# Hybrid trunk on one core: small plain-precision products as stacked parts in one single-rate product, norm sums from parts in two passes

## The chip, the cores and the metric

The kernel runs on one core of a Trainium2 chip. The time is that of the device for one execution, in microseconds (us); the number compared is the median of several executions. A profile is one further execution, recorded by the hardware profiler.

A core has engines that run side by side, each through its own list of instructions in order: TensorE (PE: matrix products into PSUM, with weight loads, PEld), VectorE (DVE), ScalarE (ACT), GpSimd (POOL) and SyncE (SP, which here issues the transfers). They wait for one another by semaphores.

## The reference

One layer of a hybrid trunk, for a prompt of 256 tokens with 16 learned meta tokens ahead of it, and for 8 sample tokens, which continue from given states. All in float32, width 2048:

```python
def decoder_layer(x, pos, s_ret, s_hg, prompt, ...):
    x = layer_norm(ALPHA * x + 0.5 * swiglu(x, f1_g, f1_u, f1_d), ln1_g, ln1_b)
    m, s_ret, s_hg = token_mixer(x, pos, s_ret, s_hg, prompt, w_in, lb, hg_norm_g, w_out)
    x = layer_norm(ALPHA * x + m, ln2_g, ln2_b)
    x = layer_norm(ALPHA * x + 0.5 * swiglu(x, f2_g, f2_u, f2_d), ln3_g, ln3_b)
    return x, s_ret, s_hg

# token_mixer: ten projections of x, then two branches
#   retention: 8 heads of 256, per-head decay; S_new = decay * S + k_dec^T v, and o = (q k^T * D) v + q_dec S
#   HGRN2: 16 heads of 128, forget gate f per feature, k = 1 - f;
#          S_new = exp(b_last) * S + k_dec^T v, and o likewise with the products of the gates
# y = sigmoid(a_r) * norm(o_r) * silu(g_r) + sigmoid(a_h) * norm(o_h) * silu(g_h);  return y @ w_out, s_ret, s_hg
```

The outputs are the tokens after the layer and the states of both branches, for the prompt and for each sample. The first 16 tokens of the prompt (the meta tokens) are computed as a chunk of their own, and are left out of the token output.

## The kernel before, in words

Features lie on the 128 partitions and tokens in the columns: 280 columns (16 meta, 256 prompt, 8 sample), or 264 where the meta tokens are no longer needed. `T` is 280, `TL` 264, `LP` 272.

**Products.** A plain float32 product shows as two records in the profile, one of float32r operands as one record; the latter is called single rate here. The kernel splits a value x in an upper part hi, which ACT makes as a copy cast to float32r, and a lower part lo = x - hi, which DVE makes as float32r (`split`, L188 to L190). `dense` (L175) makes each block of a weight product from three single-rate products, hi·hi, hi·lo and lo·hi (L182 to L184). Its weights come in units of 8 blocks of 128x128: `stream` (L143) issues the load of a unit on SP's queue, ACT casts it to `whi` (L159), DVE subtracts to `wlo` (L160); three units are in flight. `sums` (L192, L195) adds over the partitions in two passes, from an upper and a lower part, with a matrix of ones.

**Stages.** ffn 1 (up, down), then the first layer norm, the mixer, the product with `w_out` and the second norm, ffn 2, the third norm.

**Norms.** `Norm` gathers the residual in 16 tiles `d`. `shift` (L277) takes the mean of the first tile over its partitions, the product `pc` (L280), as an approximate mean that is subtracted from every tile; it is called from a hook after block k = 6 of the second output group. The running sums of d and its square are tiles `ls1` and `ls2` (`ls` in the profile), which `stats` (L310) adds over partitions in two products `p1` and `p2` (L313, L314). For norms 1 and 2 the next stage's first group of products (`first`, L322) starts with the values that are not yet normalised; `stats` is called from a hook after its block k = 4, and `normalise` (L343) rewrites `xh` and `xl` (L350, L351) behind it. The third norm ends in `finish`.

**Mixer.** For each unit u = 0 to 7 the groups of projections run, and between their blocks `pump` (after every k) takes steps of two generators, `mix_hg` (two HGRN2 heads) and `mix_ret` (one retention head). A `yield n` says how many k's to wait for the next step. In `mix_hg`, keys and values are transposed; the 16 meta tokens' keys and values go to `km` (L735) and `vm` (L656), tiles of 128 rows that are zero below row 16, and their state is the plain product `pst<-vm,km` (L751). Two chunks of 128 follow (L752, L753). In `mix_ret`, the last 24 tokens' values are in `vt2`; the states (`psr`, L852) are single rate already, and their third block of 24 tokens is one product in which parts stand below one another (`ks2`, `vs2`: rows 0, 32 and 64). The output `por` (L897) is the sum of three products with the scores: two blocks of 128 tokens and a third, `vt2` with `scr2`, of 16 columns. Values are centred (`centre`, L789) between.

**Order.** TensorE runs in the order in which the program is written. DVE and ACT are ordered by a scheduler by priorities and its own estimates, so a step of the mixer may stand behind weight splits or steps of the other branch on them. All transfers of weights, states and tables are issued by SP.

Of the kernel before, what the change touches and what calls it, by code (L numbers as in the profile page):

```python
# [10 lines left out]
F32 = mybir.dt.float32  # L11
# [90 lines left out]
def trunk(ctx: ExitStack, tc: tile.TileContext, A, O):  # L102
# [127 lines left out]
    class Norm:  # L230
# [5 lines left out]
        def __init__(self, which, n, whole, lead):  # L236
# [4 lines left out]
            if lead:  # L241
                self.bs = lnb[:, which - 1]
                split(self.bs[:, 0, :], self.bs[:, 1, :], self.b)

        def row(self, name):
            return row_tile(name)[:, : self.n]

# [29 lines left out]
        def shift(self):  # L277
            n = self.n
            pc = mx_bank("pc")
            nc.tensor.matmul(pc[:, :n], ones, self.d[0], start=True, stop=True)  # L280
# [29 lines left out]
        def stats(self):  # L310
            n = self.n
            p1, p2 = mx_bank("p1"), mx_bank("p2")
            nc.tensor.matmul(p1[:, :n], ones, self.s1, start=True, stop=True)  # L313
            nc.tensor.matmul(p2[:, :n], ones, self.s2, start=True, stop=True)  # L314
            self.mean = self.row("lnc")
            nc.scalar.mul(self.mean, p1[:, :n], 1.0 / D)
            var = self.row("lnq")
            mul(var, self.mean, self.mean)
            nc.vector.scalar_tensor_tensor(out=var, in0=p2[:, :n], scalar=1.0 / D, in1=var, op0=ALU.mult, op1=ALU.subtract)
            self.r = rsqrt(self.row, var, 1.0, (eps_h if self.whole else eps_l))  # L320

        def first(self, block, outs):  # L322

            n = self.n

            def hook(k):
                if k == 4:
                    self.stats()
# [12 lines left out]
            return ys  # L341
# [54 lines left out]
    def ffn(i, block, w_dn, which, before=None):  # L396
# [3 lines left out]
        with tc.tile_pool(name=f"h{i}", bufs=1) as hp:  # L400
# [23 lines left out]
            for m in range(KC):  # L424
                o = acc_bank(f"dn{m}")
                norm.ahead(m)
                dense(block, FC, [o], hh, hl, cols, (lambda k: k == 6 and norm.shift()) if m == 1 else None)
                norm.chunk(m, o[:, :n])
        return norm

# [34 lines left out]
    with tc.tile_pool(name="yp", bufs=1) as yp:  # L465
        yh, yl = [None] * KC, [None] * KC
        with tc.tile_pool(name="mp", bufs=1) as mp:
# [38 lines left out]
            km = tmp("km", (P, P))  # L506
            vm = tmp("vm", (P, 2, 2, P))
            vt2 = tmp("vt2", (P, 2, P))
            scr2 = tmp("scr2", (P, NMETA))


            ks2 = tmp("ks2", (P, 2, P), dt=F32R)
            vs2 = tmp("vs2", (P, 2, P), dt=F32R)
            for z in (km, vm, vt2, scr2):
                nc.gpsimd.memset(z, 0.0)
            for z in (ks2, vs2):
                nc.scalar.copy(z.rearrange("p c f -> p (c f)"), vm.rearrange("p h b f -> p (h b f)")[:, : 2 * P])
            threads = []

            def pump(_=None):  # L520
# [86 lines left out]
            NB2 = LP - 2 * P  # L607
            BLOCKS = ((0, P), (P, P), (2 * P, T - 2 * P))

            def rows_out(src, width, tag):  # L610

                scr = drp.tile([NS, width], F32, tag=tag + "d", name=tag + "d")
                nc.sync.dma_start(scr, src)
                return scr
# [11 lines left out]
            def mix_hg(u, f, k, q, v):  # L626
# [23 lines left out]
                for h in range(2):  # L650

                    pt = mx_bank("pt")
                    for b, (t0, n) in enumerate(((NMETA, P), (NMETA + P, P), (0, NMETA), (T - NMETA, NMETA))):
                        nc.tensor.transpose(pt[:n, b * P : (b + 1) * P], v[:, h, t0 : t0 + n], ident)
                    nc.scalar.copy(vt[:, h], pt[:, : 2 * P].rearrange("p (b f) -> p b f", b=2))
                    nc.scalar.copy(vm[:NMETA, h], pt[:NMETA, 2 * P :].rearrange("p (b f) -> p b f", b=2))  # L656
                    vrow.append(rows_out(vm[8:16, h, 1, :], P, f"vh{h}"))
                    yield 1
                yield 9 if u else 5
                pd = mx_bank("pd")  # L660
# [68 lines left out]
                for h in range(2):  # L729
# [5 lines left out]
                    nc.scalar.copy(km[:NMETA, :], pt[:NMETA, 2 * P : 3 * P])  # L735
# [12 lines left out]

                    S = tmp("Sh", (P, 3, P))
                    pst = mx_bank("pst")  # L750
                    nc.tensor.matmul(pst[:, 0:P], km, vm[:, h, 0, :], start=True, stop=True)  # L751
                    nc.tensor.matmul(pst[:, P : 2 * P], kt[:, 0, :], vt[:, h, 0, :], start=True, stop=True)  # L752
                    nc.tensor.matmul(pst[:, 2 * P : 3 * P], kt[:, 1, :], vt[:, h, 1, :], start=True, stop=True)  # L753
                    nc.scalar.copy(S[:, 0, :], pst[:, :P])
# [33 lines left out]

            def centre(x):  # L789

                n = x.shape[1]
                m = tmp("cen", (P, n))
                nc.vector.tensor_reduce(out=m, in_=x, op=ALU.add, axis=mybir.AxisListType.X)
                nc.vector.tensor_scalar(out=m, in0=m, scalar1=1.0 / 256, scalar2=None, op0=ALU.mult)
                nc.vector.tensor_tensor(out=x, in0=x, in1=m.unsqueeze(2).to_broadcast([P, n, 256]), op=ALU.subtract)

            def mix_ret(u, q, k, v):
                vt = tmp("vtr", (P, 2, 2, P))
# [6 lines left out]
                for c in range(2):  # L805
# [7 lines left out]
                    nc.scalar.copy(vs2[third[0], c, :], vt2[:NB, c, :])  # L813
                    nc.scalar.copy(vs2[third[2], c, :], vt2[:NB, c, :])
                    sub(vs2[third[1], c, :], vt2[:NB, c, :], vs2[third[0], c, :].bitcast(F32))
                    yield 1
                    pt = mx_bank("pt")
                    for b, (t0, n) in enumerate(BLOCKS):
# [104 lines left out]
        for gn, grp in enumerate(out_groups()):  # L923
            outs = [acc_bank(f"wo{m}") for m in grp]
            norm2.ahead(grp[0])
            dense(block, KC, outs, yh, yl, slice(0, TL), (lambda k: k == 6 and norm2.shift()) if gn == 1 else None)
            for m, o in zip(grp, outs):
                norm2.chunk(m, o[:, :TL])

# [115 lines left out]
```

## Time and profile before

| | us |
|---|---|
| median of 3 runs (2813.01 to 2816.25) | 2814.84 |
| the profiled execution | 2817.09 |
| its span | 2815.0 |
| TensorE busy (22664 records) | 2797.8, 99% |
| DVE busy (2842) | 1721.1, 61% |
| ACT busy (2034) | 1354.6, 48% |
| POOL busy (42) | 4.3 |

The mean clock granted to TensorE in the profiled execution is 0.998. A line of the timeline reads: start us, length us, engine, line, operation, output tile <- input tiles, sizes, count, and in brackets the engine's idle time before it with what ended that. The length of a matmul is longer than the distance to the next start, as matmuls overlap. A line of waits reads: engine, the tile and line that waited, the tile and line waited for, us in total, times, longest us. Buffer numbers are left out of tile names. float32r is written f32 for matmuls; a plain product shows as two records (x2).

### The profile page before, as it was taken

The page shows a single profiled execution, that of the slowest core. Times are in us where ns is not written, and L with a number is a line of the kernel's source. Part 1 is how long each engine was busy: PE and PEld are TensorE (multiplying, and loading weights), DVE is VectorE, ACT ScalarE, POOL GpSimd, SP SyncE. Part 2 cuts the span into 40 slices and gives each one's busy share as a digit, 9 for nine tenths or more (in the row PEclk, how much of TensorE's full clock was granted, in tenths as well). Part 3 has the DMA queues.
Part 4 walks back from the last instruction along what each step waited for, and adds up shares of the span by engine and source line. Part 5 has one row for each costly group of instructions (what it writes and reads, how often), then busy time and mean ns, then how long its engine had stood idle before and what let it go on. Part 6 is the DMA issues. An engine that isn't in the chain of part 4 may idle for free.

```text
span 2815.0 us, 54477 instructions
## 1 busy us (share of the span) xinstructions
PE 2797.8 (99%) x22664; PEld 2765.0 (98%) x22664; DVE 1721.1 (61%) x2842; ACT 1354.6 (48%) x2034; POOL 4.3 (0%) x42
## 2 busy tenths in 40 slices
PE   9999999999999999999999999999999999999999
PEld 9999999999999999999999999999999999999998
DVE  5444444464478777777777777775884444446444
ACT  4443344433355565656565656564554444444333
POOL 0000000000000000000000000000000000000000
PEclk9999999999999999999999999999999999999999
DMA  6555555555555675757575757575555555565654
GB/s 224 172 171 168 172 172 171 168 170 173 169 175 173 226 249 177 250 175 254 175 253 175 254 174 254 175 250 172 177 179 181 184 182 180 180 183 179 181 180 140
DMA packets 154439, 536.26 MB, mean 190 GB/s; under 512 B 17680, under 2 KB 25424, under 8 KB 154192
## 3 DMA queue, kind: packets, MB, share of 16 engines
q1 hardware_dynamic: 154048, 532.50, 59.1%
q8 instruction: 177, 2.90, 0.4%
q14 instruction: 70, 0.57, 0.1%
q10 hardware_dynamic: 144, 0.29, 0.0%
HBM read 502.12 MB, written 30.61 MB: 189 GB/s over the span
## 4 chain that ended last, share of the span: by engine, by line
PE 97%; DVE 1%; ACT 1%; DMA 1%; issue 0%; SPq 0%; ACTq 0%; DVEq 0%
PE up L183 12%; PE up L184 12%; PE up L182 12%; PE dn L182 6%; PE dn L183 6%; PE dn L184 6%; PE pj_v_r L182 1%; PE pj_f L182 1%; PE pj_k_r L182 1%; PE pj_f L183 1%; PE pj_k_r L183 1%; PE pj_v_r L183 1%; PE pj_v_r L184 1%; PE pj_f L184 1%; PE pj_g_r L182 1%; PE pj_k_r L184 1%
## 5 line engine op out<-in xcount | busy, mean ns | idle before, releaser
L160 DVE TENSOR_TENSOR wlo<-raw,whi 128x1024 fp32r<-128x1024 f32 (+1 forms) x869 | 1062.5, 1223 | 896.5 <-ACT whi L159 893.4
L159 ACT CAST whi<-raw 128x1024 fp32r<-128x1024 f32 (+1 forms) x869 | 909.3, 1046 | 1159.4 <-PE up L183 487.7
L182 PE MATMUL up<-xh,whi 128*128 128x280 f32 (+1 forms) x2688 | 773.0, 288 | 1.6 <-ACT xh L189 1.6
L183 PE MATMUL up<-xl,whi 128*128 128x280 f32 (+1 forms) x2688 | 774.1, 288 | 0.2 <-DVE xl L190 0.2
L184 PE MATMUL up<-xh,wlo 128*128 128x280 f32 (+1 forms) x2688 | 773.5, 288 | 0.0
L182 PEld LDWEIGHTS up<-xh,whi 128*128 128x128 f32 x2688 | 506.7, 188 | 1.9 <-ACT xh L189 1.9
L183 PEld LDWEIGHTS up<-xl,whi 128*128 128x128 f32 x2688 | 506.4, 188 | 0.5 <-DVE xl L190 0.5
L184 PEld LDWEIGHTS up<-xh,wlo 128*128 128x128 f32 x2688 | 506.6, 188 | 0.0
L182 PE MATMUL dn<-hh,whi 128*128 128x280 f32 (+1 forms) x1376 | 397.1, 289 | 0.0
L183 PE MATMUL dn<-hl,whi 128*128 128x280 f32 (+1 forms) x1376 | 395.8, 288 | 0.0
L184 PE MATMUL dn<-hh,wlo 128*128 128x280 f32 (+1 forms) x1376 | 395.7, 288 | 0.0
L183 PEld LDWEIGHTS dn<-hl,whi 128*128 128x128 f32 x1376 | 259.0, 188 | 0.1
L182 PEld LDWEIGHTS dn<-hh,whi 128*128 128x128 f32 x1376 | 258.9, 188 | 0.1
L184 PEld LDWEIGHTS dn<-hh,wlo 128*128 128x128 f32 x1376 | 258.6, 188 | 0.0
L182 PE MATMUL pj_g_r<-xh,whi 128*128 128x264 f32 x256 | 79.1, 309 | 0.0
L183 PE MATMUL pj_i_h<-xl,whi 128*128 128x280 f32 x256 | 75.4, 294 | 1.7 <-DVE xl L351 1.7
L182 PE MATMUL pj_v_r<-xh,whi 128*128 128x280 f32 x256 | 76.6, 299 | 0.0
L182 PE MATMUL pj_i_h<-xh,whi 128*128 128x280 f32 x256 | 75.3, 294 | 0.7 <-ACT xh L350 0.7
L182 PE MATMUL pj_g_h<-xh,whi 128*128 128x264 f32 x256 | 75.7, 296 | 0.0
L182 PE MATMUL pj_q_r<-xh,whi 128*128 128x264 f32 x256 | 75.4, 294 | 0.0
L182 PE MATMUL pj_k_r<-xh,whi 128*128 128x280 f32 x256 | 75.2, 294 | 0.0
L184 PE MATMUL pj_i_h<-xh,wlo 128*128 128x280 f32 x256 | 75.1, 293 | 0.0
(359 smaller groups left out, 5221.3 us busy)
## 6 DMA issues: line engine op xcount, KB each, us to landing
raw<-in_w_up SPq DMA_DIRECT2D x343, 512.0 KB, 3.4
raw<-in_w_in SPq DMA_DIRECT2D x320, 512.0 KB, 3.6
raw<-in_w_dn SPq DMA_DIRECT2D x172, 512.0 KB, 3.5
smr<-in_sr SPq DMA_DIRECT2D x32, 512.0 KB
out_srs<-smr SPq DMA_DIRECT2D x32, 512.0 KB, 4.5
raw<-in_w_out SPq DMA_DIRECT2D x32, 512.0 KB, 3.4
smh<-in_sg SPq DMA_DIRECT2D x16, 512.0 KB, 3.7
out_sgs<-smh SPq DMA_DIRECT2D x16, 512.0 KB, 4.0
```

What stands on the lines that cost most here:

```text
L159: nc.scalar.copy(hi[:, j0:j1, :], raw[:, j0:j1, :])
L160: nc.vector.tensor_tensor(out=lo[:, j0:j1, :], in0=raw[:, j0:j1, :], in1=hi[:, j0:j1, :].bitcast(F32), op=ALU.subtract)
L182: nc.tensor.matmul(o, wh, h, start=k == 0, stop=False)
L183: nc.tensor.matmul(o, wh, l, start=False, stop=False)
L184: nc.tensor.matmul(o, wl, h, start=False, stop=k == nk - 1)
```

## The change

It replaces plain float32 products by float32r ones in three places.

- **HGRN2's meta state** (`pst<-vm,km`, 16 times). `vm` and `km` become float32r tiles in which three blocks of 16 rows stand at rows 0, 32 and 64. Values: upper, lower, upper part; keys: upper, upper, lower part. One single-rate product over the 128 rows is then hi·hi + lo·hi + hi·lo. The parts are written by two new helpers: two ACT copies and one DVE subtraction each, from PSUM. The last 16 tokens' values, from which the samples' rows are sent out, get a tile of their own, `vsm`.
- **Retention's third output block** (`por`, 16 times). The scores become a stacked float32r tile `sc2`; the values are `vs2`, which served only the states before and is written again after `centre`. `centre` of the last block goes over 24 rows, not 128.
- **Norm sums.** `shift` and `stats` make parts of d, ls1 and ls2 (`parts`: an ACT copy and a DVE subtraction each, into the tiles rv, rr, rt and lnq) and add them in two single-rate passes. `shift` is called after k = 9, not 6, and `stats` after k = 5, not 4. `finish` is as before.

Four memsets leave POOL; five tiles are zeroed by ACT copies from a zero tile, where it was two. The lines of the changed kernel are shifted: L743 becomes L761, L751 L769, L556 L561.

```diff
+        def parts(self, x, *names):
+            hilo = [rp.tile([P, T], F32R, tag=name, name=name)[:, : self.n] for name in names]
+            split(*hilo, x)
+            return hilo
...
         def shift(self):
             n = self.n
             pc = mx_bank("pc")
-            nc.tensor.matmul(pc[:, :n], ones, self.d[0], start=True, stop=True)
+            sums(pc[:, :n], self.parts(self.d[0], "rv", "rr"))
...
             p1, p2 = mx_bank("p1"), mx_bank("p2")
-            nc.tensor.matmul(p1[:, :n], ones, self.s1, start=True, stop=True)
-            nc.tensor.matmul(p2[:, :n], ones, self.s2, start=True, stop=True)
+            sums(p1[:, :n], self.parts(self.s1, "rv", "rr"))
+            sums(p2[:, :n], self.parts(self.s2, "rt", "lnq"))
...
             def hook(k):
-                if k == 4:
+                if k == 5:
                     self.stats()
...
-                dense(block, FC, [o], hh, hl, cols, (lambda k: k == 6 and norm.shift()) if m == 1 else None)
+                dense(block, FC, [o], hh, hl, cols, (lambda k: k == 9 and norm.shift()) if m == 1 else None)
...
+            vsm = tmp("vsm", (P, 2, P))
...
+            km = tmp("km", (P, P), dt=F32R)
+            vm = tmp("vm", (P, 2, P), dt=F32R)
             ks2 = tmp("ks2", (P, 2, P), dt=F32R)
             vs2 = tmp("vs2", (P, 2, P), dt=F32R)
-            for z in (km, vm, vt2, scr2):
-                nc.gpsimd.memset(z, 0.0)
-            for z in (ks2, vs2):
-                nc.scalar.copy(z.rearrange("p c f -> p (c f)"), vm.rearrange("p h b f -> p (h b f)")[:, : 2 * P])
+            sc2 = tmp("sc2", (P, NMETA), dt=F32R)
+            for z in (km, vm, ks2, vs2, sc2):
+                z = z if len(z.shape) == 2 else z.rearrange("p c f -> p (c f)")
+                nc.scalar.copy(z, qdh[:, 0, : z.shape[1]])
...
+            def upper_lower_upper(out, x):
+                n = x.shape[0]
+                nc.scalar.copy(out[:n], x)
+                nc.scalar.copy(out[64 : 64 + n], x)
+                sub(out[32 : 32 + n], x, out[:n].bitcast(F32))
+
+            def upper_upper_lower(out, x):
+                n = x.shape[0]
+                nc.scalar.copy(out[:n], x)
+                nc.scalar.copy(out[32 : 32 + n], x)
+                sub(out[64 : 64 + n], x, out[:n].bitcast(F32))
...
-                    nc.scalar.copy(vm[:NMETA, h], pt[:NMETA, 2 * P :].rearrange("p (b f) -> p b f", b=2))
-                    vrow.append(rows_out(vm[8:16, h, 1, :], P, f"vh{h}"))
+                    nc.scalar.copy(vsm[:NMETA, h, :], pt[:NMETA, 3 * P :])
+                    vrow.append(rows_out(vsm[8:16, h, :], P, f"vh{h}"))
+                    upper_lower_upper(vm[:, h, :], pt[:NMETA, 2 * P : 3 * P])
...
-                    nc.scalar.copy(km[:NMETA, :], pt[:NMETA, 2 * P : 3 * P])
+                    upper_upper_lower(km, pt[:NMETA, 2 * P : 3 * P])
...
-                    nc.tensor.matmul(pst[:, 0:P], km, vm[:, h, 0, :], start=True, stop=True)
+                    nc.tensor.matmul(pst[:, 0:P], km, vm[:, h, :], start=True, stop=True)
...
-                vts = [vt[:, 0], vt[:, 1], vt2]
+                vts = [vt[:, 0], vt[:, 1], vs2]
...
-                scrs = [scr[:, SCORES[0][0] : SCORES[1][0]], scr[:, SCORES[1][0] : c2], scr2]
+                upper_upper_lower(sc2, scr2[:NB2])
+                scrs = [scr[:, SCORES[0][0] : SCORES[1][0]], scr[:, SCORES[1][0] : c2], sc2]
...
-                centre(vt2.rearrange("p c f -> p (c f)").unsqueeze(1))
+                vlast = vt2.rearrange("p c f -> p (c f)")[:NB]
+                centre(vlast.unsqueeze(1))
+                upper_lower_upper(vs2.rearrange("p c f -> p (c f)"), vlast)
```

The scheduler gives DVE another order at these places. First, DVE in unit 0, around the second head's keys: `smr` are retention's sample states, `on_h` the first head's normalised output, `smh` HGRN2's sample states, `wlo` weight splits. Before:

```order
L160 TENSOR_TENSOR wlo_10280<-raw_10278,whi_10279 128x8x128
L873 SCALAR_TENSOR_TENSOR smr<-vbr,k_r,smr 128x256 x4
L198 TENSOR_TENSOR on_h<-on_h,rr 128x264
L743 SCALAR_TENSOR_TENSOR smh<-vbh,fk,smh 128x128 x5
L160 TENSOR_TENSOR wlo_10326<-raw_10324,whi_10325 128x8x128
L743 SCALAR_TENSOR_TENSOR smh<-vbh,fk,smh 128x128 x3
L198 TENSOR_TENSOR q<-q,pj_q_h_9943 128x264
L756 SCALAR_TENSOR_TENSOR Sh<-Sh,T_9658,pst 128x128
```

and of the changed kernel, DVE at the same place:

```order
L160 TENSOR_TENSOR wlo_10312<-raw_10310,whi_10311 128x8x128
L892 SCALAR_TENSOR_TENSOR smr<-vbr,k_r,smr 128x256 x4
L198 TENSOR_TENSOR on_h<-on_h,rr 128x264
L204 TENSOR_TENSOR km<-ptk,km 16x128
L761 SCALAR_TENSOR_TENSOR smh<-vbh,fk,smh 128x128 x8
L198 TENSOR_TENSOR q<-q,pj_q_h_9973 128x264
L774 SCALAR_TENSOR_TENSOR Sh<-Sh,T_9680,pst 128x128
```

The subtraction for km stands behind on_h, and the weight split that stood among the smh rows has moved behind them. Second, DVE at the start of the mixer, where the first normalisation begins: `lnc` is the mean, `lnq` the variance and one of the parts' tiles, `lbt` and `mxl` rows of the forget gate's bound. Before:

```order
L160 TENSOR_TENSOR wlo_8743<-raw_8741,whi_8742 128x8x128
L201 TENSOR_TENSOR mxl<-lbt 128x16
L488 RECIPROCAL mxl<-mxl 128x16
L198 TENSOR_TENSOR lb<-lbt,mxl 128x16
L490 TENSOR_SCALAR olb<-lb 128x16
L160 TENSOR_TENSOR wlo_8773<-raw_8771,whi_8772 128x8x128
L198 TENSOR_TENSOR lnq<-lnc 128x280
L204 TENSOR_TENSOR d_5920<-d_5920,lnc 128x280
L319 SCALAR_TENSOR_TENSOR lnq<-p_8713,lnq 128x280
```

and of the changed kernel, DVE again:

```order
L190 TENSOR_TENSOR rr<-ls_5970,rv 128x280
L160 TENSOR_TENSOR wlo_8759<-raw_8757,whi_8758 128x8x128
L201 TENSOR_TENSOR mxl<-lbt 128x16
L493 RECIPROCAL mxl<-mxl 128x16
L190 TENSOR_TENSOR lnq<-ls_5971,rt 128x280
L198 TENSOR_TENSOR lb<-lbt,mxl 128x16
L495 TENSOR_SCALAR olb<-lb 128x16
L160 TENSOR_TENSOR wlo_8789<-raw_8787,whi_8788 128x8x128
L160 TENSOR_TENSOR wlo_8819<-raw_8817,whi_8818 128x8x128
L198 TENSOR_TENSOR lnq<-lnc 128x280
L204 TENSOR_TENSOR d_5920<-d_5920,lnc 128x280
L324 SCALAR_TENSOR_TENSOR lnq<-p_8731,lnq 128x280
```

The lower parts of both sums have come in, and two weight splits, not one, stand between them and the mean's first use. Between that use and the last `xl` row stand nine splits before and eight now. Third, DVE around norm 1's pc, before:

```order
L160 TENSOR_TENSOR wlo_5987<-raw_5985,whi_5986 128x8x128
L255 SCALAR_TENSOR_TENSOR d_5920<-xl_0_108,dn_5754 128x280
L256 SCALAR_TENSOR_TENSOR d_5920<-xh_0_107,d_5920 128x280
L308 COPY xlg_0_5962<-lnb 128x1
L307 COPY xhg_0_5961<-lnb 128x1
L160 TENSOR_TENSOR wlo_6017<-raw_6015,whi_6016 128x8x128
L204 TENSOR_TENSOR d_5920<-d_5920,lnc 128x280
```

and of the changed kernel:

```order
L160 TENSOR_TENSOR wlo_5992<-raw_5990,whi_5991 128x8x128
L260 SCALAR_TENSOR_TENSOR d_5920<-xl_0_108,dn_5754 128x280
L261 SCALAR_TENSOR_TENSOR d_5920<-xh_0_107,d_5920 128x280
L313 COPY xlg_0_5976<-lnb 128x1
L312 COPY xhg_0_5975<-lnb 128x1
L160 TENSOR_TENSOR wlo_6022<-raw_6020,whi_6021 128x8x128
L190 TENSOR_TENSOR rr<-d_5920,rv 128x280
L204 TENSOR_TENSOR d_5920<-d_5920,lnc 128x280
```

The lower part rr stands behind the split that was ahead of the subtraction of lnc.

More of the change, by code (lines that the diff above doesn't have):

```diff
@@ L504, in trunk @@
             nc.gpsimd.memset(qdr, 0.0)
-            km = tmp("km", (P, P))
-            vm = tmp("vm", (P, 2, 2, P))
+            vsm = tmp("vsm", (P, 2, P))
             vt2 = tmp("vt2", (P, 2, P))
             scr2 = tmp("scr2", (P, NMETA))
+            km = tmp("km", (P, P), dt=F32R)
+            vm = tmp("vm", (P, 2, P), dt=F32R)
             ks2 = tmp("ks2", (P, 2, P), dt=F32R)
             vs2 = tmp("vs2", (P, 2, P), dt=F32R)
-            for z in (km, vm, vt2, scr2):
-                nc.gpsimd.memset(z, 0.0)
-            for z in (ks2, vs2):
-                nc.scalar.copy(z.rearrange("p c f -> p (c f)"), vm.rearrange("p h b f -> p (h b f)")[:, : 2 * P])
+            sc2 = tmp("sc2", (P, NMETA), dt=F32R)
+            for z in (km, vm, ks2, vs2, sc2):
+                z = z if len(z.shape) == 2 else z.rearrange("p c f -> p (c f)")
+                nc.scalar.copy(z, qdh[:, 0, : z.shape[1]])
             threads = []
@@ L789, in centre @@
             def centre(x):
-                n = x.shape[1]
-                m = tmp("cen", (P, n))
+                np_, n = x.shape[0], x.shape[1]
+                m = tmp("cen", (P, n))[:np_]
                 nc.vector.tensor_reduce(out=m, in_=x, op=ALU.add, axis=mybir.AxisListType.X)
                 nc.vector.tensor_scalar(out=m, in0=m, scalar1=1.0 / 256, scalar2=None, op0=ALU.mult)
-                nc.vector.tensor_tensor(out=x, in0=x, in1=m.unsqueeze(2).to_broadcast([P, n, 256]), op=ALU.subtract)
+                nc.vector.tensor_tensor(out=x, in0=x, in1=m.unsqueeze(2).to_broadcast([np_, n, 256]), op=ALU.subtract)
             def mix_ret(u, q, k, v):
@@ L812, in mix_ret @@
                     split(vs[:, 0, :, f], vs[:, 1, :, f], vt[:, :, c, :])
-                    nc.scalar.copy(vs2[third[0], c, :], vt2[:NB, c, :])
-                    nc.scalar.copy(vs2[third[2], c, :], vt2[:NB, c, :])
-                    sub(vs2[third[1], c, :], vt2[:NB, c, :], vs2[third[0], c, :].bitcast(F32))
+                    upper_lower_upper(vs2[:, c, :], vt2[:NB, c, :])
                     yield 1
@@ L925, in trunk @@
             norm2.ahead(grp[0])
-            dense(block, KC, outs, yh, yl, slice(0, TL), (lambda k: k == 6 and norm2.shift()) if gn == 1 else None)
+            dense(block, KC, outs, yh, yl, slice(0, TL), (lambda k: k == 9 and norm2.shift()) if gn == 1 else None)
             for m, o in zip(grp, outs):
```

## The prediction

> **What bounds the kernel now.** I read the page's busy times, its chain, TensorE's waits, the granted clock around the longest of them, and then, in the timeline, each place that the change touches.
>
> ```profile
> PE 2797.8 (99%) x22664; PEld 2765.0 (98%) x22664; DVE 1721.1 (61%) x2842; ACT 1354.6 (48%) x2034; POOL 4.3 (0%) x42
> ...
> PE 97%; DVE 1%; ACT 1%; DMA 1%; issue 0%; SPq 0%; ACTq 0%; DVEq 0%
> ```
>
> TensorE is busy for 99% of the span and is 97% of the chain. So a product made shorter shortens the program by as much, unless TensorE meets a wait behind it, and a wait that is put before TensorE lengthens the program by as much. The waits of before, by what is waited for (us in total, times, longest):
>
> ```profile
> PE pd L195 <- ACT prodsmh L189: 2.7, 2, 2.0
> PE pj_i_h L183 <- DVE xl L351: 1.7, 2, 0.9
> PE pst L751 <- ACT km L735: 1.2, 1, 1.2
> PE pd L195 <- DVE prodvbh L190: 1.2, 1, 1.2
> ```
>
> They lie between 842 and 963 us, where the first normalisation and the first mixer unit meet. A wait there can cost more than its length, as the granted clock shows (columns: stretch, us, busy and count of PE, PEld, DVE, ACT, POOL, then PE clock, DMA share, GB/s):
>
> ```profile
> 846.00:851.00 5.00, 5.00 (x29) 4.95 (x29) 4.59 (x12) 2.69 (x4) 0.00 (x0) 0.66 0.35 108
> 860.00:865.00 5.00, 4.93 (x24) 4.52 (x25) 4.15 (x11) 1.11 (x2) 0.00 (x0) 0.66 0.27 96
> 934.00:940.00 6.00, 4.78 (x38) 4.56 (x37) 5.97 (x14) 5.89 (x13) 0.00 (x0) 1.00 0.74 285
> 961.00:967.00 6.00, 4.55 (x21) 4.15 (x22) 5.61 (x13) 1.93 (x5) 0.00 (x0) 0.72 0.29 91
> ```
>
> At 0.66 over 5 us, and 0.72 over 6 us, TensorE loses 5×0.34 = 1.7 and 6×0.28 = 1.7 us: three times after waits that add up to about 2 us. After the single wait of 1.22 us at 935 it loses nothing.
>
> **What the products save.** The plain products are two records each, a single-rate one is one. Prices are from start to start, since the matmuls overlap.
>
> ```profile
> 814.37 0.64 PE L313 MATMUL p<-ls,ones 128*128 128x280 f32 x2
> ...
> 815.45 0.29 PE L183 MATMUL pj_f<-xlg,whi 128*128 128x282 f32 x1
> ...
> 815.70 0.29 PE L182 MATMUL pj_f<-xhg,whi 128*128 128x282 f32 x1
> ...
> 908.06 0.98 PE L852 MATMUL psr<-vs,ks 128*128 128x256 f32 x7
> 908.88 0.29 PE L182 MATMUL pj_f<-xh,whi 128*128 128x280 f32 x1
> 909.65 0.38 PE L751 MATMUL pst<-vm,km 128*128 128x128 f32 x2
> 909.88 0.39 PE L752 MATMUL pst<-vth,kth 128*128 128x128 f32 x2
> ...
> 948.04 0.29 PE L897 MATMUL por<-scr,vt 128*128 128x16 f32 x2
> 948.18 0.31 PE L622 MATMUL por<-ident,osr 128*128 128x128 f32 x1
> 948.25 0.37 PE L182 MATMUL pj_q_r<-xh,whi 128*128 128x264 f32 x1
> 948.46 0.28 PE L183 MATMUL pj_q_r<-xl,whi 128*128 128x264 f32 x1
> ```
>
> A single-rate pass of 280 columns takes (815.70 − 815.45)/2 = 0.125 us, of 256 columns (908.88 − 908.06)/7 = 0.12. The two statistics products and one such pass behind them fill 1.08 us, so one product is (1.08 − 0.125)/2 = 0.48 and two passes of it 0.25: 0.22 saved, rounded. Seven norm sums (pc of three norms, p1 and p2 of two; the finish keeps its own) make −1.5 us. A pst product is 0.23, half of it 0.11; 16 of them −1.8. At 948 two records of por, a transposition and a projection pass (0.12) fill 0.42, so a record is some 0.10; 16 por −1.6. Together −4.9 us, if single rate holds for 128 and 16 columns. No row of before shows single rate below 256 columns; the bounds are nothing saved (0) and a time in proportion to the columns (0.06 for pst, 16×0.05 us more). I take one record for two, nearest to the 256-column row.
>
> **The norms' parts.** d's upper part (rv) is made by ACT, its lower (rr) by DVE, and rr stands behind the weight split that was already ahead of the subtraction of lnc. Of norm 1:
>
> ```profile
> 559.43 0.63 PE L280 MATMUL pc<-d,ones 128*128 128x280 f32 x2
> ...
> 559.81 1.23 DVE L160 TENSOR_TENSOR wlo<-raw,whi 128x1024 fp32r<-128x1024 f32 x1 [0.85 <-ACT whi L159]
> ...
> 560.96 0.44 DVE L204 TENSOR_TENSOR d<-d,lnc 128x280 f32<-128x280 f32 x1
> ```
>
> and of norm 3:
>
> ```profile
> 2564.66 0.61 PE L280 MATMUL pc<-d,ones 128*128 128x264 f32 x2
> ...
> 2565.08 1.23 DVE L160 TENSOR_TENSOR wlo<-raw,whi 128x1024 fp32r<-128x1024 f32 x1 [0.89 <-ACT whi L159]
> 2566.22 0.43 DVE L204 TENSOR_TENSOR d<-d,lnc 128x264 f32<-128x264 f32 x1
> ```
>
> With the hook three blocks later, norm 1's pass over rv starts at 559.43 + 9×0.13 = 560.6 and the one over rr is due at 560.7. rr takes the place of the row at 560.96, and is ready at 560.96 + 0.44 = 561.4: a wait of 0.7 us. In norm 3 it is due at 2564.66 + 9×0.12 + 0.12 = 2565.9 and ready at 2566.65: 0.8 us. The bounds are 0 (the split could come first) and 1.2, one split more. In norm 2 the split that rr stands behind comes some rows earlier, ahead of the last residuals, and pc three blocks later than now, so I cost that wait at nothing; without this cover it is 0.8 more. pc later by 1.1 us makes lnc later by as much; behind it stand only DVE's residuals, which the weight blocks of a whole group cover.
>
> The first normalisation is the other place. The statistics come one k later, 12 passes or 1.5 us, and the third weight split of the order piece now stands ahead of DVE's first use of the mean:
>
> ```profile
> 815.48 0.45 DVE L198 TENSOR_TENSOR lnq<-lnc 128x280 f32<-128x280 f32 x1 [0.26 <-ACT lnc L316]
> ...
> 817.12 1.03 ACT L159 CAST whi<-raw 128x1024 fp32r<-128x1024 f32 x1
> ...
> 818.37 1.22 DVE L160 TENSOR_TENSOR wlo<-raw,whi 128x1024 fp32r<-128x1024 f32 x1
> ...
> 859.98 0.50 PE L195 MATMUL pd<-prodsmh,ones_r 128*128 128x512 f32 x1 [2.05 <-ACT prodsmh L189]
> ```
>
> So this chain is late by 1.5 to 2.7 us at its start, and gets one split (1.2 from start to next row) back, since one fewer then stands among its rows: 0.3 to 1.5 at its end, the xl rows and the products behind pd, which is what TensorE waits for at 842 to 861. The extra lower parts (rr and lnq, 0.45 each) stand before it, in the stretch that waits for p1 in any case. I take +1.2, near the upper end because the order shows the split ahead; and since DVE decides here, the 0.4 us that norm 1's p1 and p2 save is lost. Norm 2's statistics are late likewise, but no wait of before lies at 2053 to 2094, so they cost nothing; if the 1.5 us were not covered there, that would be the price.
>
> **The stacked parts of km.** One more ACT copy, and a DVE subtraction that stands where DVE is busy:
>
> ```profile
> 934.67 1.22 DVE L160 TENSOR_TENSOR wlo<-raw,whi 128x1024 fp32r<-128x1024 f32 x1
> 935.81 1.67 DVE L873 SCALAR_TENSOR_TENSOR smr<-vbr,k_r,smr 128x256 f32<-128x256 f32 x4
> 937.39 0.43 DVE L198 TENSOR_TENSOR on_h<-on_h,rr 128x264 f32<-128x264 f32 x1
> 937.74 1.40 DVE L743 SCALAR_TENSOR_TENSOR smh<-vbh,fk,smh 128x128 f32<-128x128 f32 x5
> ```
>
> ```profile
> 935.16 0.24 ACT L735 COPY km<-ptk 16x128 f32<-16x128 f32 x1
> ...
> 935.45 0.49 PE L751 MATMUL pst<-vm,km 128*128 128x128 f32 x2 [1.22 <-ACT km L735]
> ...
> 946.16 0.28 PE L184 MATMUL pj_q_r<-xh,wlo 128*128 128x264 f32 x1
> ```
>
> In the order the subtraction of unit 0's second head follows on_h at 937.39, so it starts at 937.74 and, at the 0.24 of ACT's row of that size, ends at 938.0. pst is then released at 938.05 and not at 935.45: +2.6 us, a wait of 3.8 in all. The bounds are 0 (subtraction early) and 3.9 (one split more ahead). A wait of 2.05 at 859.98 stands in front of a stretch at 0.66, so I add 1.7 us of half clock; bounds 0 and 1.7. The weight split at 939, which now stands behind all eight smh rows and the states, is that of pj_q_r, whose first row with it TensorE reached at 946.16, some 6 us after the split's end; smh's and the states' rows put it 3 us later, and TensorE's own delay of 2.6 widens the gap again: covered.
>
> The other 15 km have room:
>
> ```profile
> 1006.84 0.25 ACT L735 COPY km<-ptk 16x128 f32<-16x128 f32 x1
> ...
> 1018.17 0.38 PE L751 MATMUL pst<-vm,km 128*128 128x128 f32 x2
> ```
>
> 11.3 us between copy and product, against DVE rows of 1.2 to 1.7. This cover hides their copies and subtractions, as the still longer way from the values to pst hides vm's, and the stretch from scores to por hides sc2's and vs2's (the added work of all four on DVE, 48 rows of at most 0.45, is 22 us of its 1094 idle us). POOL's four memsets fewer and ACT's three zero copies more fall in front of the mixer, outside TensorE's waits: nothing. SP's rows are the same.
>
> A rule to weigh: the Trainium skill, "TensorE: Matmul & The Clock Gate", Part 1, has the clock halved after at least one idle window of about 3.4 us, in windows that run freely, and given back after a busy one. By the 2.05 us at 859.98 the trace does not need so long a gap, though its half-clock stretches are about as long as the page's window. By the rule a wait of 3.8 us fills a whole window only by luck of phase, and the sum would be 1.7 lower; that is the third rival below.
>
> **The sum.** Products −4.9, of which 0.4 is lost: −4.5. Waits: norm 1 +0.7, norm 3 +0.8, first normalisation +1.2, km +2.6, half clock +1.7: +7.0. Net +2.5 us. The profiled execution took 2817.09 (span 2815.0 and 2.1 around it), so the change would give 2819.6 there; the median of the runs, 2814.84, lies 2.25 below the profiled one, and the forecast against it is 2817.3. A measurement of this kernel tells about 0.2% (5.6 us) from no change, so this is no change.
>
> **Rivals.** 1. Slower: a single-rate product of 128 or 16 columns takes as long as the two records it replaces. For it: no such row exists in before. Against: records of 16 columns and of 128 take nearly the same 0.10 to 0.11, so a record seems to be a fixed price here, and one is removed. Then 3.4 us are not saved: 2820.7. It decides if the new pst records start more than 0.2 apart.
> 2. Slower: the halved clock also follows the new waits of 0.7 and 0.8 us at the norms, 1.7 each: 2820.7, and with a long wait in norm 2 2822. For it: two waits of 0.70 and 1.17 us (961) were enough together. Against: 1.22 alone was not.
> 3. No change, less: km's wait comes, but not its half clock: 2815.6.
> 4. Faster: the subtractions run before the rows they stand behind matter, km and norms wait for nothing. Then −4.5 + 1.2: 2811.5; if one of the three half-clock stretches goes besides, 2809.8, and with the first normalisation covered as well 2808.6, beyond the 2809.2 that is −0.2%. Against: the order pieces show the place of each, and DVE runs its rows in order.
>
> **How the numbers follow.** Forecast 0.50 (own range 2815 to 2820, since its bounds are 0.3 to 1.5 at the first normalisation and 0 to 1.2 at each norm), rival 1 0.13, rival 2 0.14, rival 3 0.14, rival 4 0.09. Slower than 2820.4 are most of 1 and 2 and the upper end of the forecast: 0.25. Faster than 2809.2 is only rival 4 at its end: 0.05. Within 0.2%: 0.70. For 8 in 10 the range reaches from rival 4, 2811.5, to rival 2 with some more, 2822.5.
>
> **What would show it.** pst and por with one record for vm,km and vs2,sc2, each some 0.11; pc and p with two passes of 0.13; TensorE waiting for rr at 560 and 2566 by 0.7 to 0.9; at u=0's second head a wait for DVE's km of 3 to 4 us and a stretch under full clock behind it; the waits for prodvbh and xl longer by about 1. Wrong would make me: a new wait in a later unit, where a DVE row of 11 us or more of backlog stands before km, or a split of weights that comes late in the changed order.

## The result

The changed kernel takes 2819.3 us (median of 16 runs, 2817.08 to 2822.14), the kernel before 2813.78 us (16 runs, 2811.85 to 2816.25): ratio 1.0019, 95% interval 1.0012 to 1.0026, which is +5.5 us, from 3.4 to 7.3. That is just inside the 0.2% called no change and inside the range; the forecast of +2.5 us had the sign, and was 3 us short.

The two profiled executions differ by less, 2817.41 us against 2817.09. The one of before lies above all 16 runs of its kernel, the one of the changed kernel near the low end of its own; why is told below. The page of the changed kernel:

```profile
span 2815.3 us, 54597 instructions
...
PE 2793.7 (99%) x22632; PEld 2758.6 (98%) x22632; DVE 1737.1 (62%) x2897; ACT 1375.5 (49%) x2124; POOL 3.4 (0%) x38
```

TensorE is busy 4.1 us less than before and 90 rows have come to ACT, 55 to DVE. Its waits:

```profile
PE pst L769 <- DVE km L204: 4.0, 1, 4.0
PE pd L195 <- DVE prodvbh L190: 2.8, 2, 1.7
PE pj_i_h L183 <- DVE xl L356: 2.1, 5, 0.9
PE pc L195 <- DVE rr L190: 1.2, 2, 0.7
...
PE pd L195 <- ACT prodsmh L189: 0.9, 2, 0.7
```

Three are new or longer: km from 1.2 to 4.0 and now on DVE, rr at pc, and prodvbh from 1.2 to 2.8 (while prodsmh fell from 2.7 to 0.9: the second part is now the later one). The rows behind them, norm 1 first (two views, of TensorE and of DVE):

```profile
560.03 0.29 PE L195 MATMUL pc<-rv,ones_r 128*128 128x280 f32 x1
560.89 0.40 PE L195 MATMUL pc<-rr,ones_r 128*128 128x280 f32 x1 [0.57 <-DVE rr L190]
```

```profile
559.25 1.23 DVE L160 TENSOR_TENSOR wlo<-raw,whi 128x1024 fp32r<-128x1024 f32 x1 [0.84 <-ACT whi L159]
560.39 0.45 DVE L190 TENSOR_TENSOR rr<-d,rv 128x280 fp32r<-128x280 f32 x1
```

rr starts the moment the weight split lets DVE go. Then unit 0's second head:

```profile
935.30 1.66 DVE L892 SCALAR_TENSOR_TENSOR smr<-vbr,k_r,smr 128x256 f32<-128x256 f32 x4
936.88 0.42 DVE L198 TENSOR_TENSOR on_h<-on_h,rr 128x264 f32<-128x264 f32 x1
937.34 0.28 DVE L204 TENSOR_TENSOR km<-ptk,km 16x128 fp32r<-16x128 f32 x1
```

```profile
937.77 0.30 PE L769 MATMUL pst<-vm,km 128*128 128x128 f32 x1 [4.05 <-DVE km L204]
937.90 0.54 PE L770 MATMUL pst<-vth,kth 128*128 128x128 f32 x2
```

The granted clock at the same places as before, of the changed kernel:

```profile
846.00:851.00 5.00, 3.42 (x22) 2.80 (x22) 5.00 (x13) 2.49 (x5) 0.00 (x0) 1.00 0.38 108
860.00:865.00 5.00, 3.44 (x27) 3.40 (x28) 5.00 (x13) 1.29 (x3) 0.00 (x0) 1.00 0.45 148
934.00:944.00 10.00, 6.23 (x39) 6.10 (x43) 8.18 (x23) 6.47 (x15) 0.00 (x0) 0.83 0.61 236
961.00:969.00 8.00, 6.15 (x46) 5.58 (x45) 7.25 (x17) 5.27 (x10) 0.00 (x0) 1.00 0.41 141
```

A half-clock stretch follows km's wait, 10×0.17 = 1.7 us. But the stretches that the profile of before had at 846, 862 and 964 are gone, though the waits ahead of them are as long in sum. That is part of why these two executions come out alike: the one of before lies 3.3 us above its kernel's median, of which the stretches at 862 and 964 cost 1.0 to 1.4 us each, and the one of the changed kernel lies 1.9 us below its own.

### The profile page after: what moved, and what is told of

It is laid out like the page before. It is cut to its first block, busy times and chain, and to the rows that moved or that the text cites. A ratio compares the mean times of both kernels' runs of the same rounds, so it can differ in the third digit from the quotient of the medians.

```text
span 2815.3 us, 54597 instructions
## 1 busy us (share of the span) xinstructions
PE 2793.7 (99%) x22632; PEld 2758.6 (98%) x22632; DVE 1737.1 (62%) x2897; ACT 1375.5 (49%) x2124; POOL 3.4 (0%) x38
## 4 chain that ended last, share of the span: by engine, by line
PE 97%; DVE 1%; ACT 1%; DMA 1%; issue 0%; SPq 0%; DVEq 0%
PE up L183 12%; PE up L184 12%; PE up L182 12%; PE dn L182 6%; PE dn L183 6%; PE dn L184 6%; PE pj_v_r L182 1%; PE pj_f L182 1%; PE pj_k_r L182 1%; PE pj_v_r L183 1%; PE pj_f L183 1%; PE pj_k_r L183 1%; PE pj_f L184 1%; PE pj_g_r L182 1%; PE pj_v_r L184 1%; PE pj_k_r L184 1%
## 5 line engine op out<-in xcount | busy, mean ns | idle before, releaser
L183 PE MATMUL pj_v_r<-xl,whi 128*128 128x280 f32 x256 | 74.6, 292 | 0.0
```

Of the source, the lines that this page charges most:

```text
L183: nc.tensor.matmul(o, wh, l, start=False, stop=False)
```

## The experiments

Medians and ratios are against the kernel before, run on the same chip in the same rounds. Each of these ratios is uncertain by about 2.5 us.

### The products alone, the norms alone

The products alone: the changed kernel with

```diff
-            sums(pc[:, :n], self.parts(self.d[0], "rv", "rr"))
+            nc.tensor.matmul(pc[:, :n], ones, self.d[0], start=True, stop=True)
...
-                if k == 5:
+                if k == 4:
...
-(lambda k: k == 9 and norm.shift())
+(lambda k: k == 6 and norm.shift())
```

and p1 and p2 likewise.

> The changed kernel with the norm sums plain again and the hooks at k = 6 and 4. My theory (TensorE is shortened by 0.10 a product and lengthened by each wait for a DVE part): 32 products make -3.3 us, the wait for km's subtraction in unit 0 +2.8, half clock behind it 0 to +1.4, the late rlo at pvr up to +1.6: -0.5 to +2.5 us against the kernel before. Rival (the norms make the loss of 5.5 us, the products only gain): -3.3 us.

Measured 2816.13 us against 2814.45: 1.0007 (0.9998 to 1.0015), +1.9 us or so. The profile has km's wait of 4.3 us, with a stretch at 0.71 behind it over 934 to 944, and no other new wait over 0.5 us in the mixer. The rival of a pure gain falls; my sum for these parts (−3.4 + 2.6 + 1.7 = +0.9) lies in the interval.

The norms alone, on the kernel before (the same lines the other way):

> The kernel before with the norm sums from parts and the hooks at k = 9 and 5 alone. My theory: norm 1's pc +0.6 net, norm 3's +0.7, norm 2 -0.6, the first normalisation +0.9: +1.6 us, and no wait of 4 us in unit 0. Rival (the norms make the loss): +5 us or more, most of it between 815 and 870 us.

Measured 2817.13 us: 1.0011 (1.0002 to 1.0019), +3.1 us. The forecast's terms for the norms add up to +1.6, inside the interval. But km's wait, which I expected as in before, was longer in this profile, and the release was ACT's:

```profile
PE pst L756 <- ACT km L740: 3.0, 1, 3.0
```

```profile
932.41 1.06 ACT L875 ACTIVATE smr<-smr 128x1024 f32<-128x1024 f32 x1 [1.64 <-DMA smr<-in_sr]
...
937.64 0.24 ACT L740 COPY km<-ptk 16x128 f32<-16x128 f32 x1
```

ACT's row for retention's sample state waited 1.64 us for its load, and km's copy stands behind that row on ACT. In the first profile of before the same row ran at 929.93 without a wait. The load before it, for which ACT waited in both, was used 4.7 us after its issue there (911.99 to 916.71), and 5.8 here (912.74 to 918.52), and the load of this row was issued at 925.95, there at 924.16. So the length of km's wait goes with how fast a transfer lands; that this differs between executions of one program too, the second profile of the changed kernel shows below. The two halves, +1.9 and +3.1, add up to 5.0 of the 5.5 (by the ratios; the medians differ by 1.7 and 2.7).

### km's parts early, on both engines and on DVE alone

```diff
-                    upper_upper_lower(km, pt[:NMETA, 2 * P : 3 * P])
+                    with tc.high_priority():
+                        upper_upper_lower(km, pt[:NMETA, 2 * P : 3 * P])
```

> The changed kernel with km's parts at high priority, so that DVE makes the subtraction among the smr rows and not behind on_h. My theory: pst's wait goes from 4.0 back to about 1.2 us and the half-clock stretch behind it goes: 2.8 to 4.1 us faster than the changed kernel, +1.4 to +2.7 against before. Rival (the wait is hidden by another, the run's half-clock stretches decide): within 1.5 us of the changed kernel.

Measured 2811.62 us against 2814.45: 0.9991 (0.9982 to 1.0000). This is 2.8 us faster than before and some 8 us faster than the changed kernel, twice what I expected. In its profile pst waits 0.5 us and the granted clock stays at 1.00 over 934 to 944, although the sample state's load was late again, by 2.17 us at the same row. km's copies still stand behind that row, but no longer behind a weight cast and the next sample state's row. That profiled execution took 2814.26 us, near the top of its eleven runs and 3.2 us less than the profiled one of the changed kernel, so the rest of the 8 us is seen in no trace. To see which engine's order does it, only the subtraction was moved:

```diff
-                sub(out[64 : 64 + n], x, out[:n].bitcast(F32))
+                with (tc.high_priority() if n == NMETA and out.shape[1] == P else ExitStack()):
+                    sub(out[64 : 64 + n], x, out[:n].bitcast(F32))
```

> The changed kernel with km's DVE subtraction alone at high priority; ACT's two copies stay behind the smr row on ACT, as km's copy does in the kernel before. If the subtraction's place on DVE is what costs (2.6 us and the half clock behind), this is 3 to 4 us faster than the changed kernel, +1.5 to +2.5 against before, and the wait of pst is that of before, 1.2 us, or 3.0 where the sample states land late. If ACT's place behind smr costs as much, it stays 3 to 4 us slower than the run with both early (0.9991 of before).

Measured 2815.87 us against 2814.69: 1.0004 (0.9995 to 1.0013), +1.2 us. By the medians DVE's place is worth 5.5 − 1.2 = 4.3 us, with an uncertainty of about 3. That is the number which the forecast had for it (2.6 and 1.7 of half clock), but the profile does not show these two terms gone:

```profile
PE pst L770 <- DVE km L204: 2.4, 1, 2.4
```

```profile
934.00:944.00 10.00, 7.64 (x56) 6.70 (x55) 8.82 (x23) 7.63 (x17) 0.00 (x0) 0.83 0.67 258
```

The wait fell by 1.6 us, and the half clock behind it stayed. So the agreement with 2.6 and 1.7 is luck as far as this trace goes. ACT's place is worth some 4 us more by the medians; in the profiles the wait goes from 2.4 to 0.5 us and the half clock behind it goes. In the kernel before the same was done for its one copy:

```diff
-                    nc.scalar.copy(km[:NMETA, :], pt[:NMETA, 2 * P : 3 * P])
+                    with tc.high_priority():
+                        nc.scalar.copy(km[:NMETA, :], pt[:NMETA, 2 * P : 3 * P])
```

> The kernel before with km's one ACT copy at high priority, nothing else. If pst's wait in unit 0 (1.2 us in the profile of before, 3.0 with the norms alone changed) costs the kernel before too, it is 1.2 to 3 us faster than before: 0.9989 to 0.9996. If it costs only what the one profile shows and another wait follows, within 1 us of before.

Measured 2813.01 us against 2814.69: 0.9994 (0.9985 to 1.0002). The sign is as expected, but no change lies in the interval. The waits of pst are not in its profile any more.

### The products with km early

The products alone, with km's parts at high priority as above:

> Plain norm sums as before, the stacked products, and km's parts at high priority. My theory: the 32 products' -3.3 us are left whole, or down to -1.7 if pvr's waits for rlo stay: 0.06% to 0.12% faster than before. Rival: another wait of unit 0 takes the place of km's, within 1 us of before.

Measured 2810.01 us against 2814.45: 0.9985 (0.9976 to 0.9993), 4.4 us faster. That is 2.8 more than the kernel before gains from km alone (−1.7 and −4.4), near the 3.4 of the forecast for the products, and uncertain by 3 or so. And 2811.62 − 2810.01 = 1.6 us is what the norms' parts with hooks at 9 and 5 cost once km is out of the way: the forecast's sum for them.

### The wait filled with work

```diff
+                    for _ in range(18 if (u, h) == (0, 1) else 0):
+                        nc.tensor.matmul(pst[:, 0:P], ones, ident, start=True, stop=True)
                     nc.tensor.matmul(pst[:, 0:P], km, vm[:, h, :], start=True, stop=True)
```

> The changed kernel with 18 plain products of 128 columns (4.0 us), whose results are overwritten, ahead of unit 0's second pst, where TensorE waits 4.0 us for km. If the wait trips the half clock behind it, which costs 1.3 us in the profile, the stretch goes and the time falls by 1.3 us or more against the changed kernel. If the wait alone costs, the time stays within 0.5 us of the changed kernel (+5.5 us against before).

Measured 2817.1 us against 2814.69: 1.0007 (0.9999 to 1.0016), +2.4 us, against +5.5 of the changed kernel. 18 useless products made it about 3 us faster; the intervals touch at 1.0012 to 1.0016, so the size is loose. The trace shows why it can be so:

```profile
934.79 4.18 PE L770 MATMUL pst<-ident,ones 128*128 128x128 f32 x36
938.91 0.33 PE L771 MATMUL pst<-vm,km 128*128 128x128 f32 x1
```

```profile
934.00:944.00 10.00, 10.00 (x91) 9.54 (x93) 9.22 (x25) 7.69 (x17) 0.00 (x0) 1.00 0.76 283
```

km is as late as before, TensorE is busy through the 4 us, and the granted clock stays at 1.00, where it was 0.83. By the lag (how much later the same projection rows start than in the first profile of before), the stretch behind km costs 1.4 us in the changed kernel's first profile; the other half of the 3 us is not explained.

### The hooks placed for the parts

```diff
-(lambda k: k == 9 and norm.shift())
+(lambda k: k == 12 and norm.shift())
...
-                if k == 5:
+                if k == 4:
```

on the norms alone:

> The kernel before with the norm sums from parts alone, but the hooks at k = 12 for pc and k = 4 for the statistics, as in the placed run. If the norms' loss (+3.1 us with hooks at 9 and 5) is the waits behind the hooks, it is gone: TensorE's seven sums save 1.5 us, of which 0.4 is lost before 861 us, so -1.0 us against before, 4 us faster than the norms with hooks at 9 and 5. If the parts themselves cost (their DVE and ACT rows push unit 0's sample states), it stays 1 us or more slower than before.

Measured 2813.76 us against 2813.79: 0.9998 (0.9989 to 1.0007). The loss of 3.1 us is gone; of the expected gain of 1.0 the interval can't tell. The profile has no wait for rr, and prodsmh at 2.0, prodvbh at 1.2 and km at 1.2 as in before. So the parts cost next to nothing where they are ready, and most of what cost was where they were asked for. Part of the difference is km's wait, 3.0 us in the profile of the norms alone and 1.2 here. And on the run with km's parts early:

> The run with km's parts early, and besides the hook of pc at k = 12 and that of the statistics back at k = 4. Theory: the waits for rr at pc go (-1.2 us) and the first normalisation starts 1.5 us earlier, some -1 us at its end: 2 us faster than the run with km's parts early alone, 0.9984 of before. Rival: the first normalisation is bound by its DVE rows, not its start, and only the 1.2 us go.

Measured 2808.32 us (8 runs, 2806.98 to 2808.72) against 2814.69: 0.9975 (0.9964 to 0.9985). This beats both kernels, by 6.4 us and by some 12. Its waits, and the clock in unit 0:

```profile
PE pd L195 <- ACT prodsmh L189: 2.7, 2, 2.0
PE pj_i_h L183 <- DVE xl L356: 2.2, 3, 1.0
...
PE pd L195 <- DVE prodvbh L190: 1.2, 1, 1.2
```

```profile
860.00:865.00 5.00, 4.96 (x40) 4.92 (x41) 4.93 (x12) 1.66 (x3) 0.00 (x0) 1.00 0.21 86
934.00:944.00 10.00, 10.00 (x97) 8.88 (x96) 10.00 (x29) 7.49 (x16) 0.00 (x0) 1.00 0.82 261
```

The waits for km and rr are gone; those for the first normalisation are the ones of before. That the first normalisation starts earlier pays at its end: between 817 and 862 us this run gains 1.9 us on the one with km early alone.

### Both kernels once more

> The changed kernel unaltered, for a second profile and its time beside the others on one chip: +5.5 us against before again. If the stretches of half clock are set by the kernel, the one at 939 us is there again and none at 862 and 964; if by the phase of the execution, the places differ. The waits (4.0 for km, 0.6 and 0.7 for rr) are the same, but km's longer by up to 2 us if the sample state's load lands late.

Measured 2819.61 us against 2813.79: 1.0019 (1.0010 to 1.0028). km's wait was 4.8 us, 0.8 longer than in the first profile, and the sample state's row waited 0.61 for its load, where it had not (it ran 7.0 us after the load's issue, in the first profile 6.0). The half clock was again behind km's wait and not at 862 or 964.

> The kernel before unaltered, for a second profile. If the half-clock stretches go by phase, those at 846, 862 and 964 us of the first profile are not all there; the waits are 2.0 at 860, 0.7 and 1.2 at 961 to 963 and 1.2 at 935 again, the last longer if the sample state's load lands late.

One run, 2815.32 us. The waits at these places are those of the first profile to 0.1 us; one of 0.8 us at 1170 is new. The clock is not:

```profile
860.00:865.00 5.00, 5.00 (x30) 4.82 (x29) 4.07 (x11) 1.46 (x3) 0.00 (x0) 0.70 0.19 75
934.00:944.00 10.00, 9.17 (x78) 8.43 (x79) 9.66 (x27) 7.07 (x15) 0.00 (x0) 1.00 0.73 253
961.00:969.00 8.00, 6.84 (x52) 6.64 (x52) 8.00 (x19) 3.14 (x5) 0.00 (x0) 1.00 0.29 93
```

In the first profile the last stretch was at 0.79, here it is at 1.00, behind the same waits of 0.7 and 1.2 us.

## Why the prediction was right or wrong

**The products' price: right.** One record takes the place of two. In the changed kernel the records at 909 and 952 read

```profile
909.25 0.22 PE L769 MATMUL pst<-vm,km 128*128 128x128 f32 x1
...
951.70 0.27 PE L916 MATMUL por<-sc,vs 128*128 128x16 f32 x1
951.83 0.32 PE L639 MATMUL por<-ident,osr 128*128 128x128 f32 x1
```

and wherever a pst or a por stands, the projection products behind it come 0.10 to 0.11 us earlier than in before. This step is seen at each of the later units. Rival 1 (short single-rate products at the price of two records) is out.

**The norms' parts: right in place, a little less in size.** The waits at norms 1 and 3 were 0.57 and 0.66 us for 0.7 and 0.8; none at norm 2. Between 527 and 567 us the changed kernel falls back 0.63 us, and 0.73 at norm 3; the forecast's net was 0.5 and 0.6. The first normalisation: pd's second pass starts at 861.56 and not at 860.55, 0.94 later once the lag at its start is taken off, against 1.2.

**km: right in place and size in the profile.** 4.05 us of wait for 3.8, and a half-clock stretch of 1.7 for 1.7 (1.4 by the lag). The run that undoes DVE's place alone gains the predicted 4.3 us without losing these two terms in its trace, so it does not confirm the split. What the step did not have is the row ahead of it: km's copy on ACT stands behind the sample states' rows, and with them behind loads that land up to 7.0 us after their issue in these profiles. The longer waits of 4.3 and 4.8 in other executions go with these loads (0.19 and 0.61 us of waiting at the row that had none). The kernel of the norms alone has only ACT's copy of km, and waits 3.0 us for it. This was in the trace of before (the wait of 1.2 us was for ACT's km, and a copy of 0.24 us behind a row of 1.05), and I took it as given.

**What the sum lacked.** In the traces there is one more loss: in each of five later units the second pass of a retention head's norm now waits for its lower part, and the lag against before jumps by 0.24 us in four of them and by 0.67 in one (1757 us). In the changed kernel, DVE and TensorE in unit 2 (of DVE the row of rlo stood at 1334.18 in before, and the second pass at 1334.85):

```profile
1333.43 1.23 DVE L160 TENSOR_TENSOR wlo<-raw,whi 128x1024 fp32r<-128x1024 f32 x1
1334.58 0.43 DVE L190 TENSOR_TENSOR rlo<-sqr,rhi 128x264 fp32r<-128x264 f32 x1
...
1335.06 0.39 PE L195 MATMUL pvr<-rlo,ones_r 128*128 128x264 f32 x1
```

The weight split ahead of rlo starts 0.4 us later than it did. That is 1.6 us in all which I had put at nothing, on the ground that DVE has 1094 idle us. This cover is the step that failed: an average of idle time does not say what stands ahead of the next row. One of the signs that the prediction names, a split of weights that comes late, is what came. The runs place it: these waits are there with the products alone and not with the norms alone; with km's subtraction alone at high priority they stay, and in the three runs with km's ACT copies at high priority too (both parts changed, products alone, placed) none is left. Which row then moves the split is not shown.

**What the base was.** The sum was made against one execution of before with three half-clock stretches. The one at 846 costs nothing, since TensorE waits for DVE until 861 anyway; the other two cost 1.0 to 1.4 us each by the lags. The sum took them as fixed in both kernels. They are not. Behind the wait of 2.0 us at 860 the stretch was there in three profiles (before twice, before with km early) and not in four (products alone, products with km early, norms with the hooks placed, placed). Behind the pair of waits of 0.7 and 1.2 us a hundred us later it was there in one profile of before and not in the other. Behind km's waits of 4.0 to 4.8 us it was there in all three, behind one of 2.4 too, and behind one of 3.0 (norms alone) not. So waits of 2 to 3 us trip the half clock in some executions, and those of 4 in all that were recorded.

The records of the granted clock show most of what decides. Between 10 and 2795 us of the thirteen profiles a stretch lasts 3.41 us (twice two follow one another), and the stretches of one execution start whole multiples of 3.413 us apart: in the first profile of before at 846.73, 860.38 and 962.78, with 4 and 30 such steps between them. So each execution has a grid of its own. Cut on its grid, the wait of 2.05 us at 860 reads in before and in the placed run:

```profile
856.96:860.38 3.42, 1.37 (x10) 0.95 (x8) 3.17 (x11) 1.61 (x4) 0.00 (x0) 1.00 0.64 175
860.38:863.79 3.41, 3.34 (x15) 3.14 (x15) 3.21 (x9) 0.00 (x0) 0.00 (x0) 0.50 0.32 132
```

```profile
855.25:858.66 3.41, 2.17 (x18) 1.96 (x17) 3.12 (x10) 1.50 (x4) 0.00 (x0) 1.00 0.47 155
858.66:862.08 3.42, 2.55 (x17) 2.19 (x18) 3.38 (x10) 1.07 (x3) 0.00 (x0) 1.00 0.48 153
```

In before the whole wait falls into one window, which leaves TensorE idle for 2.05 us, and the half clock follows; in placed the grid splits the same wait into 1.25 and 0.87, and it does not. So it is in all seven: whole in one window in the three profiles with a stretch, split in the four without. Over all profiles in that range, all 12 windows at full clock that leave TensorE idle for 1.84 us or more are followed by a stretch, none with less than 1.27 is, and of those between 4 of 21 are; what decides there stays open. The 3.0 us of the norms alone fell into two windows, as 1.82 and 1.14. A wait over 3.7 us leaves one window with more than 1.84 wherever the grid lies, so by this estimate km's waits of 4 us could not escape, and waits of about 2 us go by the phase of the execution.

The Trainium skill, "TensorE: Matmul & The Clock Gate", Part 1, has windows that run freely and make the outcome depend on their phase. That agrees with these grids, and with a stretch that comes and goes behind the same wait. Its limit of about 3.4 us of idle time is longer than the 2.05 us that were enough here.

**The other rivals.** Rival 3 (no half clock behind km) did not come about. Nor did rival 2: neither profile of the changed kernel has a stretch near 560 or 2566 us, where the waits are 0.57 and 0.66. Rival 4 did not either, but what it describes, parts that are ready when they are asked for, is what the run with km early and the hooks placed has, and its 2808.32 us is near the 2808.6 at that rival's end.

**Direction and size.** Slower was right, by km, the norms and the first normalisation as forecast. Of the 3 us that the forecast was short, 1.6 are the late second passes by the trace. The rest fits km's wait lengthened by late loads (0.3 to 1.0 us over the 3.8 in the profiles at hand) and the half clock's chances. Both profiled executions of the changed kernel are among the 6 of its 27 with a mean granted clock of 0.999, which took 2817.4 us in the mean; the 16 at 0.998 took 2819.9. So the usual execution has lost more to the clock than the profiled ones, at places that no trace shows, and the longer time goes with it. How the last 1 to 2 us are shared stays open; the measurement's own interval is 4 us wide. Against the kernel before, +5.5 lies just above the forecast's own range (2815 to 2820 against 2814.84, so +0.2 to +5.2). That the wide range holds it owes something to luck: its upper end was made for rival 2, which did not come about.

## What to carry to other kernels

Splitting an operand into parts moves work from a busy engine to idle ones, but each part is a row in a queue: read which rows stand ahead of it there, and ask for the part some blocks later, or write it at high priority, before counting the gain. Here the same products and sums gave +5.5 us or −6.4 us, by the place of two hooks and one helper. Where TensorE must wait, a wait of a few us can cost its length and some 1.4 us more by the clock, so that a stretch filled with useless work may be cheaper than an idle one.

## What the runs showed of the hardware

- Replacing the two records of a plain product by one single-rate record saved 0.10 to 0.11 us at 128 columns and at 16; a single-rate pass of 280 takes 0.125. So for such short products only the number of records counts.
- The half-clock stretches of one execution lie on a grid of 3.413 us. They followed every window of it in which TensorE was idle for 1.84 us or more (12 of 12), 4 of 21 with 1.27 to 1.82, and none with less. The same program had one at 964 us in one profile (0.79 over 961 to 969) and not in the next (1.00).
- A 512 KB load of sample states landed 4.1 to 6.0 us after its issue in executions of nearly the same program, and the one behind it up to 7.0 us after; in the profile with the norms alone, km's copy on ACT and the product on TensorE, which use nothing of these states, ran about 2 us later behind them.
